# Two reorderings in a hybrid trunk kernel: PSUM copy and decay steps of the CD projections, and the last gated tile of the delta-rule mixer

## The chip, the core and the metric

The kernel runs on one core of a Trainium2 chip. The metric is the device time of one execution in microseconds. The kernel before took 2537.91 us (median of 3 runs, 2536.88 to 2539.83). Engines are named as in the profile: PE multiplies matrices, DVE is the vector engine, ACT the scalar engine, POOL the GpSimd engine, SP issues the DMAs. L840 is line 840 of the kernel.

## What is computed

The reference is a trunk of two residual layers over 1024 tokens of width 1024. Layer 0 mixes with gated delta-rule heads and short gated convolutions (AB), layer 1 with HGRN2 heads and dilated window attention (CD); each layer ends in a SwiGLU block. Two pieces bear on the change. The output of the delta rule is normalised and gated before the output projection, and the gate of HGRN2 is turned into a decay and a key:

```python
o_a = (rms_norm(o_a, norm_g) * silu(z)).reshape(b, t, DN_VW)   # mixer AB
return concatenate([o_a, o_b], axis=-1) @ w_out
f_gate = lb + (1.0 - lb) * sigmoid(hf)                          # mixer CD
log_f = log(f_gate)
k_in = (1.0 - lb) * sigmoid(-hf)
```

With x the projected gate, the kernel uses E = exp(-x), log_f = ln(1 + lb E) - ln(1 + E), and k_in from E and exp(-ln(1 + E)).

## The kernel before

**Arithmetic.** Tokens run along the free axis in two halves of 512. Every large float32 product is made of three matmuls (L135, L136, L137, or L129, L130 and then L132 where the third kind is put last): each operand is split into a high part, a cast on ACT (L102), and the rest, a subtraction on DVE (L103). The third kind reads the low part of the weights, so it is the one that needs the DVE subtraction.

**CD products (`Local.pair`).** The projections of layer 1 are done two output blocks at a time (a "pair" f, 3 to 15) by a seven-product scheme in place of eight. On PE a pair is `p1(f)`, `p2(f)`, `end21(f-1)`, `end12(f-1)`, `p6(f)`, `p5(f)`, `p7(f)`, 12 matmuls each, 84 in all. The order of PE, DVE, ACT, POOL and SP is the order in which the code is written. Each pair needs four weight units: `part_a` for the next pair's p1 and p2 (a11, a12), `part_b` from the weight sums that POOL forms (L335, L336), `part_c` and `part_d` from raw blocks that POOL then combines further (L340, L341). So the DVE split of `part_a(f+1)`, late in pair f, is what the last four matmuls of `p1(f+1)` (L132) wait for.

`copy22(f)` (L878, ACT) copies the PSUM bank x[f], complete when p7(f) ends, into a buffer c; `add22` (L884, DVE) adds another bank to it, and only after the copy may `end21(f)` accumulate on into that bank. The results are then turned by the rotary table: ACT copies the halves crosswise (L859, L860), POOL multiplies (L861), DVE multiplies (L863) and adds (L871). `add11` is L898, `add12` L927, the copies that release the banks are L371 (gt) and L398 (u).

**Decay steps.** For pairs f from 4 to 11 one block of an earlier gate projection goes through `decay(f, 0..7)`: load (SP, L824), clamp (DVE, L829), E = exp(-x) (ACT, L831), two logarithms into c and dy (ACT, L835 and L836, with a load of ACT's function table ahead, attributed to L835), their difference (DVE, L840), exp(-dy) (ACT, L842, again with a table load), a product (DVE, L844), and a running sum (DVE, L847). Steps 0 and 1 are in pair f; before the change steps 2 and 3 are at the end of pair f, step 4 (L840) in pair f+1 behind `part_b`, steps 5 to 7 later in pair f+1. The buffers c come from a pool of two that copy22 and the decay steps share.

**AB, end of the mixer.** `short_conv` projects the convolution branch and calls `tick()` after seven of the eight k-steps of a projection; `tick` counts down and resumes the generator `delta`, which walks through the eight chunks of the delta rule and says with `yield n` how many ticks pass before it is resumed. Its last tiles are `gated(6)` and `gated(7)`: L1851 to L1856 form the scale, L1858 scales the tile (DVE, into dgo), L1861 transposes it on PE in four matmuls, L1865 gates it (DVE), L1866 stores it to DRAM. When short_conv is done, `next(steps)` runs the first 12 matmuls of the output projection of half 0 (k-blocks 4 to 7), then `delta` is run to its end, then the projection goes on. Only PE's order is written out there; a scheduler orders the other engines.

Of the kernel before, what the change touches and what calls it, by code (L numbers as in the profile page):

```python
# [55 lines left out]
def hybrid_trunk_kernel(ctx: ExitStack, tc: tile.TileContext, x_t, w_all, w_down, w_ba, vecs, c_f, c_i, c_rope, out):  # L56
# [33 lines left out]
    def psg():  # L90
        return ps.tile([P, HT], F32, tag="g", name="psg", bufs=2)
# [4 lines left out]
    def psm():  # L96
        return ps.tile([P, HT], F32, tag="m", name="psm", bufs=3)


    def split(hi, lo, src, eng=V):  # L100

        S.copy(hi, src)  # L102
        eng.tensor_tensor(lo, src, hi.bitcast(F32), op=SUB)  # L103

    def unit():

        return ring.tile([P, 2, DM], F32R, tag="w", name="w", bufs=4)
# [180 lines left out]
    class Up:  # L288
# [205 lines left out]
        def pair(self, f, b11, b21, b22, t1, t2, t3, t4):  # L494

            n = f + 1
            self.p1(f, b11)
            self.add22(f - 1)
            an = self.raw("g", n, n % 3 == 1)
            if f == 3:  # L500
                a, b, s = self.w3
                self.sums_late(a, b, s)
                self.combine(0)
                self.part_b(3, s)
                self.combine(1)
            else:
                self.part_d(f, self.a)
                bn = self.raw("u", n, n % 3 == 2)
                self.block_sums()
            self.p2(f, b21, psm())  # L510
            g = self.snap(f)
            if f == 3:
                self.part_c(3, b)
                self.part_d(3, a)
                bn = self.raw("u", n)
            if f > 3:
                self.combine(f - 2)
            self.add11(f, g)
            self.gate11(f)
            if f > 3:  # L520
                self.block_load()
            s = self.sums(an, bn)
            self.end21(f - 1, t4)
            self.part_a(n, an)
            self.sums_late(an, bn, s)
            self.end12(f - 1, b22)
            if f in (5, 7, 9, 11):
                self.block_sums()
            self.late.pop()()
            if f - 1 >= NF // 2:  # L530
                self.ask(f - 1)
            self.p6(f, t2)
            if f in (5, 7, 9, 11):
                self.block_load()
            self.p5(f, t1, psg())
            self.part_b(n, s)
            self.part_c(n, bn)
            self.a = an
            self.p7(f, t3)
# [212 lines left out]
    class Local(Up):  # L752
# [212 lines left out]
        def pair(self, f, last, b11, b21, b22, t1, t2, t3, t4):  # L965

            n = f + 1
            self.p1(f, b11, True)
            self.copy22(f - 1)
            if not last:  # L970
                an = self.raw("g", n, n % 3 == 1)
            else:
                raws = [ring.tile([P, DM], F32, tag="raw", name="raw", bufs=2),
                        self.left.tile([P, DM], F32, tag="spare", name="raw", bufs=1)]
                for raw, j in zip(raws, (8, 9)):
                    dma(raw, w_all[W_AT["cd", j]])
            self.add22(f - 1)
            self.part_b(f, self.s)
            self.sums_late(self.a, self.b, self.s)
            self.decay(f - 1, 4)  # L980
            self.p2(f, b21, psm())
            g = self.snap(f)
            self.rope22(f - 1)
            self.decay(f - 1, 5)
            self.decay(f, 0)
            self.end21(f - 1, t4)
            self.add11(f)
            self.part_c(f, self.b)
            self.rope11(f)
            self.decay(f, 1)  # L990
            self.end12(f - 1, b22)
            self.p6(f, t2)
            self.rope21(f - 1)
            self.part_d(f, self.a)
            self.decay(f - 1, 6)
            if not last:
                bn = self.raw("u", n, n % 3 == 2)
            self.add12(f - 1)
            if not last:
                self.part_a(n, an)  # L1000
            self.decay(f - 1, 7)
            self.store()
            self.p5(f, t1, psg())
            if last:
                self.lead_w = [unit(), unit()]
                for u, raw in zip(self.lead_w, raws):
                    split(u[:, 0, :], u[:, 1, :], raw)
            self.rope12(f - 1)
            if not last:
                self.s = self.sums(an, bn)  # L1010
                self.a, self.b = an, bn
            else:
                self.back = [ring.tile([P, DM], F32, tag="raw", name="raw", bufs=2) for _ in range(2)]
                for i, raw in enumerate(self.back):
                    dma(raw.rearrange("p (k t) -> p k t", k=2), self.b12[:, 2 * i:2 * i + 2, :])
            if f == 3:
                self.bounds()
            self.decay(f, 2)
            self.decay(f, 3)
            self.store()  # L1020
            self.p7(f, t3)

# [295 lines left out]
    def mixer_ab(hn, rb, hp, tr, first, later, second, close, wba, steps):  # L1318
# [102 lines left out]
        with ExitStack() as es:  # L1421
# [291 lines left out]
            def delta(yd, xd, load_al, load_cx):  # L1713
# [132 lines left out]
                def gated(c):  # L1846

                    half, cc = divmod(c, 4)
                    ss = us[c]
                    rq = sca["rq"][:, c, :]  # L1850
                    V.tensor_tensor(ss, ss, rq, op=MULT)  # L1851
                    V.tensor_tensor(ss, ss, rq, op=MULT)
                    V.tensor_scalar(ss, ss, 1.0 / P, EPS, op0=MULT, op1=ADD)
                    rr = bt("rr", [4])
                    G.tensor_tensor(rr, ss, mhalf[:, 0:4], op=ALU.pow)
                    V.tensor_tensor(rr, rr, rq, op=MULT)  # L1856
                    on = bt("dgo", bufs=1)
                    V.tensor_tensor(on, os_all[c], hb(rr), op=MULT)  # L1858
                    o = psm()
                    for h in range(4):  # L1860
                        T.transpose(o[:, h * P:(h + 1) * P], on[:, h, :], ident)  # L1861
                    szc = bt("szc", bufs=1)
                    dma(szc, scr_z[half, :, :, cc * P:(cc + 1) * P])
                    go = bt("dgo", bufs=1)
                    V.scalar_tensor_tensor(go, v4(o), vec[:, R_DNG:R_DNG + 1], szc, op0=MULT, op1=MULT)  # L1865
                    dma(catd[half][0:4, :, cc * P:(cc + 1) * P].rearrange("k p t -> p k t"), go)  # L1866
# [26 lines left out]
                        outputs(c)  # L1893
                    yield 3
                gated(6)
                yield 10
                gated(7)

            def small():


                yield 4
                step(8, 0)
                yield 12
                parts = inverses()
                yield 81
                yield from delta(*parts)
# [15 lines left out]
    def mixer_cd(hn, hp, qkd, wv):  # L1923
# [6 lines left out]
        with ExitStack() as es:  # L1930
# [30 lines left out]
            def hgrn_v(pair, w, tick, tts=range(8)):  # L1961
                def put(tt, o):
                    half, j = divmod(tt, 4)
                    if j == 0:
                        while pair and half and done_c[0] < 3:
                            next(hg_chain)
                        vts[pair, half] = hl("vt", (4, 256), 3)
                    S.copy(vts[pair, half][:, j, :], o)
                v_rows(w, tick, put, tts)
# [711 lines left out]
```

## Time and profile before

| | |
|---|---|
| median of 3 runs | 2537.91 us (2536.88 to 2539.83) |
| the profiled execution | 2542.21 us, span 2540.4 us, clock 0.998 |
| PE busy | 2516.0 us (99%), 13957 matmuls |
| DVE, ACT, POOL busy | 1690.6 (67%), 1081.0 (43%), 649.2 us (26%) |
| DMA moved | 451.48 MB, 178 GB/s on average |

A matmul's busy time in this profile (0.39 us for 512 columns) overlaps its neighbour's. What counts is the distance from one start to the next: 0.227 us where nothing is waited for. A row of the timeline gives start, length, engine, line, operation, output and inputs, and in brackets how long the engine had been idle before and what ended it.

### The profile page before, as it was taken

The numbers are of one execution on the slowest core, as the hardware profiler recorded it, in microseconds if no ns is written. First come the engines' busy times: TensorE is split into PE (matmuls) and PEld (weight loads), VectorE is DVE, ScalarE is ACT, GpSimd is POOL, SyncE is SP. The second block draws the span as 40 slices with busy tenths as digits, with TensorE's granted clock in tenths as the row PEclk, the third lists the DMA queues.
The fourth block names the chain that finished last, engine by engine and source line by source line (L and its number), as shares of the span: only waits on it lengthen the run. The fifth ranks groups of instructions, "written<-read, shape, count | busy, mean of one in ns | idle before, by whom it ended". The sixth has DMA issues, their size and how long they took to land. (4 is left out here: it accounts for less than half of the span.)

```text
span 2540.4 us, 37502 instructions
## 1 busy us (share of the span) xinstructions
PE 2516.0 (99%) x13957; PEld 2083.4 (82%) x13957; DVE 1690.6 (67%) x2858; ACT 1081.0 (43%) x1828; POOL 649.2 (26%) x557
## 2 busy tenths in 40 slices
PE   9999999999999999999999999999999999999998
PEld 7888888888888888888877889888888888888887
DVE  8887786685656565567688666566658565666554
ACT  5422113353333344344676544456645333334442
POOL 0111111343333300033466410000133343330001
PEclk9999999999999999999999999999999999999999
DMA  4435447325556588533344534576742555568753
GB/s 162 155 121 166 131 153 260 113 87 186 183 191 214 202 303 289 187 139 135 126 141 133 187 131 137 152 201 209 234 158 87 177 192 187 203 216 282 278 179 123
DMA packets 281174, 451.48 MB, mean 178 GB/s; under 512 B 49152, under 2 KB 137760, under 8 KB 280736
## 3 DMA queue, kind: packets, MB, share of 16 engines
q1 hardware_dynamic: 280992, 449.10, 53.0%
q8 instruction: 109, 1.79, 0.3%
q14 instruction: 73, 0.60, 0.1%
HBM read 304.74 MB, written 144.26 MB: 177 GB/s over the span
## 5 line engine op out<-in xcount | busy, mean ns | idle before, releaser
L103 DVE TENSOR_TENSOR w<-raw,w 128x1024 fp32r<-128x1024 f32 (+1 forms) x323 | 379.6, 1178 | 129.0 <-ACT w L102 128.5
L102 ACT CAST w<-raw 128x1024 fp32r<-128x1024 f32 (+1 forms) x323 | 306.8, 956 | 268.2 <-PE psu L137 132.9
L135 PE MATMUL psu<-hnh,w 128*128 128x512 f32 x772 | 307.7, 399 | 0.0
L137 PE MATMUL psu<-hnh,w 128*128 128x512 f32 x772 | 301.5, 391 | 0.0
L136 PE MATMUL psu<-hnl,w 128*128 128x512 f32 x772 | 301.1, 390 | 0.0
L196 POOL TENSOR_TENSOR acc<-acc,sq 128x512 f32<-128x512 f32 x52 | 79.4, 1527 | 514.4 <-ACT sq L192 514.3
L335 POOL TENSOR_TENSOR ws<-raw 128x512 f32<-128x512 f32 x54 | 70.6, 1308 | 408.9 <-DMA raw<-in_dram 257.4
L137 PEld LDWEIGHTS psu<-hnh,w 128*128 128x128 f32 x772 | 144.9, 188 | 31.0
L135 PEld LDWEIGHTS psu<-hnh,w 128*128 128x128 f32 x772 | 145.0, 188 | 29.8 <-issue 0.8
L136 PEld LDWEIGHTS psu<-hnl,w 128*128 128x128 f32 x772 | 145.2, 188 | 28.4
L103 DVE TENSOR_TENSOR w<-ws,w 128x1024 fp32r<-128x1024 f32 x51 | 64.7, 1268 | 129.6 <-ACT w L102 129.6
L103 DVE TENSOR_TENSOR hidq<-hr,hidq 128x1024 fp32r<-128x1024 f32 x72 | 82.0, 1141 | 78.7 <-ACT hidq L102 78.6
L102 ACT CAST hidq<-hr 128x1024 fp32r<-128x1024 f32 x72 | 70.3, 980 | 103.1 <-DMA hr<-ts 59.7
L135 PE MATMUL psm<-hidq,w 128*128 128x512 f32 (+1 forms) x275 | 106.1, 386 | 0.0
L136 PE MATMUL psm<-hidq,w 128*128 128x512 f32 (+1 forms) x275 | 105.8, 385 | 0.0
L137 PE MATMUL psm<-hidq,w 128*128 128x512 f32 (+1 forms) x275 | 105.8, 385 | 0.0
L341 POOL TENSOR_TENSOR raw<-raw,ws 128x512 f32<-128x512 f32 x51 | 80.6, 1581 | 60.4 <-DVE w L103 59.2
L135 PE MATMUL psu<-t4h,w 128*128 128x512 f32 x240 | 94.7, 395 | 0.6 <-ACT c L878 0.4
L861 POOL TENSOR_TENSOR sw<-sw,rope 128x512 f32<-128x512 f32 x48 | 72.3, 1506 | 89.5 <-ACT sw L860 68.0
L426 POOL TENSOR_TENSOR hid<-hid,c 128x512 f32<-128x512 f32 x44 | 62.0, 1409 | 125.8 <-ACT hid L425 125.4
L136 PE MATMUL psu<-t4l,w 128*128 128x512 f32 x240 | 93.5, 390 | 0.0
L137 PE MATMUL psu<-t4h,w 128*128 128x512 f32 x240 | 93.5, 389 | 0.0
(548 smaller groups left out, 6787.1 us busy)
## 6 DMA issues: line engine op xcount, KB each, us to landing
raw<-in_dram SPq DMA_DIRECT2D x227, 512.0 KB, 4.3
sd<-in_dram SPq DMA_DIRECT2D x44, 512.0 KB, 4.1
hid<-hid SPq DMA_DIRECT2D x88, 256.0 KB, 3.1
sd<-sd SPq DMA_DIRECT2D x44, 512.0 KB, 3.4
hr<-ts SPq DMA_DIRECT2D x40, 512.0 KB, 4.0
raw<-sd SPq DMA_DIRECT2D x40, 512.0 KB, 4.3
qk<-z SPq DMA_DIRECT2D x52, 256.0 KB, 3.2
hd<-h SPq DMA_DIRECT2D x48, 256.0 KB, 2.8
```

The lines of the kernel that those rows point to most:

```text
L102: S.copy(hi, src)
L103: eng.tensor_tensor(lo, src, hi.bitcast(F32), op=SUB)
L135: T.matmul(o, lh, rh, start=first and i == 0, stop=False, **kw)
L136: T.matmul(o, lh, rl, start=False, stop=False, **kw)
L137: T.matmul(o, ll, rh, start=False, stop=last and i == n - 1, **kw)
L196: (eng or G).tensor_tensor(a, a, q, op=ADD)
L335: G.tensor_tensor(s[:, HT:], b[:, :HT], b[:, HT:], op=ADD)
L341: G.tensor_tensor(a[:, HT:], a[:, HT:], s[:, :HT], op=SUB)
L426: G.tensor_tensor(h, h, self.c22.pop(f), op=MULT)
L861: G.tensor_tensor(sw, sw, self.table[:, 1, t], op=MULT)
```

## The change

In `Local.pair` the decay steps 2 and 3 (exp, table load, two logarithms) leave the end of pair f and come in pair f+1 right behind `copy22(f)`; step 4, the subtraction, moves ahead of the split of `part_b`. In mixer AB, `yield 10` ahead of `gated(7)` becomes `yield 100`: the ticks of short_conv run out first, and the tile comes when `delta` is run to its end.

```diff
@@ Local.pair
             self.p1(f, b11, True)
             self.copy22(f - 1)
+            self.decay(f - 1, 2)
+            self.decay(f - 1, 3)
...
             self.add22(f - 1)
+            self.decay(f - 1, 4)
             self.part_b(f, self.s)
             self.sums_late(self.a, self.b, self.s)
-            self.decay(f - 1, 4)
             self.p2(f, b21, psm())
...
-            self.decay(f, 2)
-            self.decay(f, 3)
             self.store()
             self.p7(f, t3)
@@ mixer_ab, delta
                 gated(6)
-                yield 10
+                yield 100
                 gated(7)
```

**ACT in the CD products.** This is where pair 5 ends and pair 6 begins, before the change; numbers behind names are buffers, and brackets name the engines or queues that an instruction waits for.

```order
L831 ACTIVATE dx_10042<-dx_10042 128x512
L835 ACT_TABLE_LOAD
L835 ACTIVATE c_10140<-dx_10042,lb_9574 128x512 [waits Activation_49]
L836 ACTIVATE dy_10139<-dx_10042 128x512
L878 COPY c_10169<-psu_9996 128x512 [waits DVE_49,PE_49]
L102 CAST w_10175<-ws_10135 128x1024 [waits Pool_49]
```

The same place after the change:

```order
L878 COPY c_10164<-psu_9991 128x512 [waits PE_49]
L831 ACTIVATE dx_10042<-dx_10042 128x512
L835 ACT_TABLE_LOAD [waits DVE_49]
L835 ACTIVATE c_10168<-dx_10042,lb_9574 128x512 [waits Activation_49]
L836 ACTIVATE dy_10167<-dx_10042 128x512
L102 CAST w_10176<-ws_10135 128x1024 [waits Pool_49]
```

The copy went from behind the four decay instructions to ahead of them. The wait for DVE went with the buffer: the copy now gets the buffer c that the last copy used, and the logarithm the one that the last decay used, so the table load ahead of it waits for DVE's running sum (L847) of the decay before.

**DVE in the CD products,** behind add22 of the same pair, as a difference (+ after, - before):

```order
 L863 TENSOR_TENSOR psg<-psg,rope 128x512
 L884 TENSOR_TENSOR psm<-c,psg 128x512
-L103 TENSOR_TENSOR w<-ws,w 128x1024
 L840 TENSOR_TENSOR c<-c,dy 128x512
+L103 TENSOR_TENSOR w<-ws,w 128x1024
 L871 TENSOR_TENSOR z<-psg,sw 128x128x4
 L863 TENSOR_TENSOR psm<-psm,rope 128x512
```

The decay subtraction changed places with the split of part_b. All eight decay pairs change in this way.

**PE at the end of the AB mixer,** before (psu_3863 is short_conv's last projection, psu_3956 the first output projection):

```order
L137 MATMUL psu_3863<-hnh_106,w_2669 128x512
L1861 MATMUL psm_3893<-cf_69,dgo_3891 128x128 [waits DVE_49,PE_49]
L1861 MATMUL psm_3893<-cf_69,dgo_3891 128x128 x3
L135 MATMUL psu_3863<-hnh_106,w_2669 128x512
L136 MATMUL psu_3863<-hnl_107,w_2669 128x512
L137 MATMUL psu_3863<-hnh_106,w_2669 128x512
L135 MATMUL psu_3956<-hnh_3910,w_3946 128x512
```

After (psu_3938 is the first output projection):

```order
L135 MATMUL psu_3938<-hnh_3892,w_3928 128x512
L136 MATMUL psu_3938<-hnl_3893,w_3928 128x512
L137 MATMUL psu_3938<-hnh_3892,w_3928 128x512
L1861 MATMUL psm_3959<-cf_69,dgo_3957 128x128 [waits DVE_49,PE_49]
L1861 MATMUL psm_3959<-cf_69,dgo_3957 128x128 x3
L135 MATMUL psu_3938<-hnh_3910,w_3928 128x512
```

The four transposes of gated(7) come 15 matmuls later: behind the last three of short_conv and the 12 of the output projection's first part. On DVE the gating of the tile (L1865) falls behind the convolution's output (L1537), one weight split and two operand splits; on SP its store (L1866) falls behind the convolution's store and a weight load, directly ahead of the eight loads of the residual (L176), and of the operand loads of half 1 (L1288) the third comes behind a store of the residual (L252) that it was ahead of.

## The prediction

> **What bounds the kernel now.** I read the page first, for the engine that has no room:
>
> ```profile
> PE 2516.0 (99%) x13957; PEld 2083.4 (82%) x13957; DVE 1690.6 (67%) x2858; ACT 1081.0 (43%) x1828; POOL 649.2 (26%) x557
> ```
>
> PE is busy 99% of the span and the change neither adds nor removes an instruction on any engine, so it can win only where PE stands still. The view of PE's waits has two rows at the changed places:
>
> ```profile
> PE psm L1861 <- DVE dgo L1858: 0.7, 1, 0.7
> PE psu L132 <- DVE w L103: 1.1, 4, 0.4
> ```
>
> The first is gated(7), the second the low-weight matmuls of p1 in the CD pairs. A wait row only counts what is idle beyond a matmul's modelled end, so it understates; the distance of starts tells more. The timeline of PE gives the first matmul of p1 of pairs 5, 6, 14 and 15:
>
> ```profile
> 1221.47 0.39 PE L129 MATMUL psu<-hnh,w 128*128 128x512 f32 x1
> 1240.51 0.39 PE L129 MATMUL psu<-hnh,w 128*128 128x512 f32 x1
> 1398.17 0.39 PE L129 MATMUL psu<-hnh,w 128*128 128x512 f32 x1
> 1417.21 0.39 PE L129 MATMUL psu<-hnh,w 128*128 128x512 f32 x1
> ```
>
> Pair 14 has no decay and takes 1417.21 - 1398.17 = 19.04 us, 0.2267 for each of its 84 matmuls. Pair 5 takes 19.04 too, with decay steps beside it, so these don't slow the matmuls as such. The eight pairs 6 to 13 take 157.66 us, and 8 x 19.04 = 152.32: **5.34 us are lost there**, 0.67 a pair. This is the most that the CD part can give.
>
> What sets those pairs is a round of the other engines. ACT in pair 8 (p1 begins at 1280.30):
>
> ```profile
> 1281.87 0.58 ACT L860 COPY sw<-psg 64x512 f32<-64x512 f32 x1
> 1282.48 0.63 ACT L831 ACTIVATE dx<-dx 128x512 f32<-128x512 f32 x1
> 1285.05 0.61 ACT L836 ACTIVATE dy<-dx 128x512 f32<-128x512 f32 x1
> 1285.57 0.57 ACT L878 COPY c<-psu 128x512 f32<-128x512 f32 x1
> 1287.20 1.05 ACT L102 CAST w<-ws 128x1024 fp32r<-128x1024 f32 x1 [1.06 <-POOL ws L336]
> 1289.35 0.58 ACT L860 COPY sw<-psm 64x512 f32<-64x512 f32 x1
> 1291.29 1.28 ACT L842 ACT_TABLE_LOAD   x1 [1.35 <-DVE c L840]
> 1293.12 1.03 ACT L102 CAST w<-raw 128x1024 fp32r<-128x1024 f32 x1
> ```
>
> DVE and POOL in the same pair:
>
> ```profile
> 1282.24 1.21 DVE L847 TENSOR_TENSOR_SCAN dy<-rmask,c 128x512 f32<-128x512 f32 x1
> 1284.28 0.75 DVE L863 TENSOR_TENSOR psg<-psg,rope 128x512 f32<-128x512 f32 x1
> 1286.17 0.70 DVE L884 TENSOR_TENSOR psm<-c,psg 128x512 f32<-128x512 f32 x1 [1.14 <-ACT c L878]
> 1288.29 1.23 DVE L103 TENSOR_TENSOR w<-ws,w 128x1024 fp32r<-128x1024 f32 x1 [1.42 <-ACT w L102]
> 1289.43 1.78 DVE L840 TENSOR_TENSOR c<-c,dy 128x512 f32<-128x512 f32 x1
> 1292.72 0.68 DVE L898 TENSOR_TENSOR psm<-psm,gt 128x512 f32<-128x512 f32 x1
> 1294.18 1.23 DVE L103 TENSOR_TENSOR w<-raw,w 128x1024 fp32r<-128x1024 f32 x1 [0.79 <-ACT w L102]
> 1298.90 0.69 DVE L103 TENSOR_TENSOR w<-raw,w 128x512 fp32r<-128x512 f32 x1
> 1300.76 1.23 DVE L103 TENSOR_TENSOR w<-raw,w 128x1024 fp32r<-128x1024 f32 x1
> ...
> 1285.87 1.30 POOL L336 TENSOR_TENSOR ws<-ws,raw 128x512 f32<-128x512 f32 x1
> 1287.12 1.31 POOL L340 TENSOR_TENSOR raw<-raw 128x512 f32<-128x512 f32 x1
> 1288.38 2.29 POOL L341 TENSOR_TENSOR raw<-raw,ws 128x512 f32<-128x512 f32 x1
> ```
>
> Followed forward: part_b's cast (1287.20) waits for POOL's sums; DVE splits it, then runs L840 until 1291.21; only then may ACT load the table for L842, after an idle 1.35 us; then comes part_c's cast, whose split (1294.18) DVE has waited 0.79 us for. From there DVE runs without a break to part_a's split, which ends at 1301.99. PE wants it eight matmuls after p1 began at 1299.95, at 1301.76, and got it later:
>
> ```profile
> 1301.53 0.39 PE L130 MATMUL psu<-hnl,w 128*128 128x512 f32 x1
> 1302.04 1.20 PE L132 MATMUL psu<-hnh,w 128*128 128x512 f32 x4
> ```
>
> The start is 0.28 us late; restarting and the other late spot (end21 behind the copy L878, done at 1286.14) make up the rest of the 0.67.
>
> **CD, step by step.** *Copy ahead of the decay steps.* After L860 (1282.45) the copy comes first, to 1283.02; everything in front of the second logarithm moves 0.57 later, and that ends at 1286.2 instead of 1285.66. Behind it stands part_b's cast, which waits for POOL until 1287.20 anyway: its idle 1.06 us pays for the 0.57, at no cost. L884 then runs when DVE is through with L863 (1285.03), 1.14 earlier, and end21 no longer waits for the copy.
>
> *L840 ahead of part_b's split.* It may start at 1286.25, in time in which DVE idles now. It needs 0.6 to 1.8 us: 0.69 is what a split of the same size with both inputs in SBUF takes while POOL is idle (1298.90), 1.78 what L840 takes behind POOL's L341, which itself takes 2.29 against 1.31 for L340. In either case it ends before 1288.1, ahead of the cast's end at 1288.25. L842's table load then follows L860 at 1289.94 instead of 1291.29: **1.35 us off the round.** Part_c's cast ends 1292.8 instead of 1294.15.
>
> *What is late next.* Part_b's split may be held behind L340, which L840 has pushed back: between 0 and the 1.30 us of one such POOL operation; I take 0.6, so that it ends at 1290.1. Two operations on, L898 ends 2.2 us later (as now from L840's end at 1291.21 to 1293.40), at 1292.3, still ahead of part_c's cast. At the other end, 1.30, it would be 1293.0, and 1.15 of the 1.35 would be left. So the 1.35 arrive at part_a's split. The round took 19.7 us a pair and can then do 18.3; PE needs 19.04 and becomes the bound. In pair 14 the same last stretch, fed by PE's own p6, ends this much ahead of need:
>
> ```profile
> 1416.21 1.21 DVE L103 TENSOR_TENSOR w<-raw,w 128x1024 fp32r<-128x1024 f32 x1
> 1419.03 1.07 PE L132 MATMUL psu<-hnh,w 128*128 128x512 f32 x4
> ```
>
> 1419.03 - 1417.42 = 1.6 us; a decay pair has the product L844 and the clamp L829 in that stretch as well, about 0.8 together by the split's 0.69 as the nearest size, which leaves 0.8. I expect no stall at L132, and book 5.0 of the 5.34 us, leaving 0.3 for single late starts that the pattern doesn't show. Bounds: 5.34 if nothing stays; 0 if another link of the round is as long as the one cut; below nothing only by the new wait under the rivals.
>
> A rule of the Trainium skill speaks against this place: "SBUF — State Buffer", section "Who interferes with whom", says that a DVE instruction with two SBUF inputs and a GpSimd instruction that reads SBUF exclude each other for a whole instruction. The trace agrees, with L840 at 1.78 us where 0.69 would do. By the rule the harm depends on who comes first: an L840 that gets in ahead of L336 holds the sums, and part_b's cast, by 0.69. That leaves 0.66 of the 1.35, about what PE loses per pair; it is the rival "half" below.
>
> **AB.** PE and DVE at gated(7):
>
> ```profile
> 405.84 0.74 DVE L1530 SCALAR_TENSOR_TENSOR sca<-cs,vec,sca 128x512 f32<-128x512 f32 x1
> 406.50 0.68 DVE L1858 TENSOR_TENSOR dgo<-os,rr 128x512 f32<-128x512 f32 x1
> ...
> 406.26 0.39 PE L137 MATMUL psu<-hnh,w 128*128 128x512 f32 x1
> 407.33 0.63 PE L1861 MATMUL psm<-cf,dgo 128*128 128x128 f32 x4 [0.68 <-DVE dgo L1858]
> ```
>
> The transposes start 1.07 us after the matmul ahead of them, 0.84 more than 0.227. Fifteen matmuls later PE reaches them at 406.49 + 15 x 0.227 = 409.9, and L1858, whose place on DVE is the same, ended at 407.18: **0.84 us** go. The cost of the transposes themselves stays.
>
> What moves with them is on DVE and SP. L1865 goes from 408.97 to about 412.1 behind its new neighbours, its store to 412.8, and the residual loads queued behind that store on SP move from 412.50 to about 413.2:
>
> ```profile
> 412.50 4.07 SPq L176 DMA_DIRECT2D h<-in_dram  x8
> 416.64 0.69 DVE L1312 TENSOR_TENSOR h<-h,psu 128x512 f32<-128x512 f32 x1 [0.20 <-DMA h<-in_dram]
> 431.82 1.23 DVE L103 TENSOR_TENSOR w<-raw,w 128x1024 fp32r<-128x1024 f32 x1
> 435.69 0.39 PE L135 MATMUL psg<-hnh,w 128*128 128x512 f32 x1
> ```
>
> The first addition (L1312) then starts near 417.3, in time in which DVE would wait for the next product. The operand load of half 1 that falls behind a residual store (L1288) comes perhaps 2 us later and holds DVE in order; the next weight split (431.82, ending at 433.05) serves the matmuls of 435.69, which come 0.84 earlier: 1.8 us of room. Cover lost there would cost PE the difference, at most some 0.5 us. I take 0.8 for AB, between 0.3 and 0.84.
>
> **Sum.** 5.0 + 0.8 = 5.8 us. The profiled execution took 2542.21 us, 1.81 of it outside the span of 2540.4, and becomes 2536.4. It stands 4.30 above the median of the runs; taking the same off 2537.91 gives **2532.1 us**. Whoever adds the two upper bounds gets 6.18 and 2531.7.
>
> **Rivals.**
> *Half (0.17).* DVE and POOL take back what the order gives: L840 gets in ahead of L336, part_b's cast slips by 0.69, and stalls of some 0.3 us a pair remain. For it speaks that L840's new time, 1286.25, is close to L336's start; against it that L336 starts first, at 1285.87. 5.34 / 2 + 0.8 = 3.5: 2534.4.
> *CD does nothing (0.12).* Another link, such as the raw block that feeds the sums, is equally long; then the table load waits elsewhere and L132 as before. Pair 14, whose PE loses nothing with the same loads, speaks against it. Only AB's 0.8 remain: 2537.1.
> *Slower (0.05).* The logarithm's table load now waits for DVE's running sum L847, which ends at 1283.45, and that load is due at 1283.67: 0.2 us of room. ACT works in order, so a late L847 holds part_b's cast and all behind it. Room of 1.0 ahead of the cast and the 1.35 gained have to be used up first; from an L847 that ends 2.4 us later on, each further 0.5 costs eight times 0.5: 2541. Since L847 stands right behind part_a's split, which comes earlier, not later, I give it little.
> *The forecast (0.66).* Between 2531.0 and 2533.5, with the scatter of a median of few runs of about 1 us.
>
> A measurement of this kernel can tell about 0.2% from no change, 5.1 us: the line lies at 2532.8, 0.7 above my forecast. Of the 0.66 some 0.49 falls below it, and nearly nothing of the rest: faster 0.50; same 0.46; slower 0.04. Range 2530.7 to 2535.8: it takes in the forecast's spread and the half case, and leaves out the last two.
>
> **What would show it.** Right: in pairs 6 to 13 p1 begins every 19.04 us; L842's table load follows L860 with no idle time for L840; L884 starts straight behind L863; the transposes of gated(7) start 0.23 us after the matmul ahead of them. Wrong: pairs stay above 19.3; an idle time ahead of L835's table load (by L847) or a longer one ahead of part_b's cast; L840 or part_b's split near 2.5 us; a new gap of PE between 408 and 445.

## The result, and the profile after the change

The changed kernel takes 2533.66 us (median of 18 runs, 2532.65 to 2536.38), the kernel before 2539.09 (18 runs, 2536.32 to 2544.23). The ratio is 0.998, with a 95% interval of 0.9972 to 0.9987: **5.1 us faster, between 3.3 and 7.1**.

The page of the changed kernel has the same number of instructions on PE, which is again busy for 99% of a span that is now 2531.5 us:

```profile
PE 2510.7 (99%) x13957; PEld 2083.7 (82%) x13957; DVE 1699.0 (67%) x2858; ACT 1082.0 (43%) x1828; POOL 648.4 (26%) x557
```

The timeline of PE shows the first matmul of p1 in pairs 6 and 14:

```profile
1240.29 0.39 PE L129 MATMUL psu<-hnh,w 128*128 128x512 f32 x1
1392.61 0.39 PE L129 MATMUL psu<-hnh,w 128*128 128x512 f32 x1
```

The eight decay pairs take 152.32 us, which is 8 x 19.04 to the hundredth. All of the 5.34 us are gone. This is how ACT now goes through pair 8 (p1 begins at 1278.37):

```profile
1279.68 0.59 ACT L878 COPY c<-psu 128x512 f32<-128x512 f32 x1
1280.16 0.63 ACT L831 ACTIVATE dx<-dx 128x512 f32<-128x512 f32 x1
1280.81 1.28 ACT L835 ACT_TABLE_LOAD   x1
...
1284.29 1.06 ACT L102 CAST w<-ws 128x1024 fp32r<-128x1024 f32 x1 [0.94 <-POOL ws L336]
1286.45 0.58 ACT L860 COPY sw<-psm 64x512 f32<-64x512 f32 x1
1287.05 1.28 ACT L842 ACT_TABLE_LOAD   x1
...
1292.17 0.59 ACT L398 COPY u<-psu 128x512 f32<-128x512 f32 x1 [1.05 <-PE psu L137]
```

Four things are to be seen. The copy L878 stands first, and the cast of part_b still waits 0.94 us for POOL: the copy has only used up idle time. The table load of L842 starts 0.02 us after L860 ends, with no bracket behind it: the wait of 1.35 us for L840 is gone. The table load of L835, which now waits for the running sum L847, follows L831 without a gap: the new wait costs nothing. And L398 waits 1.05 us for PE, where in the kernel before it had no wait in this pair: now PE sets the pace of the helpers. DVE and POOL in the same pair:

```profile
1279.16 1.21 DVE L847 TENSOR_TENSOR_SCAN dy<-rmask,c 128x512 f32<-128x512 f32 x1
...
1281.87 0.69 DVE L884 TENSOR_TENSOR psm<-c,psg 128x512 f32<-128x512 f32 x1
1283.39 1.42 DVE L840 TENSOR_TENSOR c<-c,dy 128x512 f32<-128x512 f32 x1 [0.82 <-ACT dy L836]
1285.38 1.66 DVE L103 TENSOR_TENSOR w<-ws,w 128x1024 fp32r<-128x1024 f32 x1 [0.57 <-ACT w L102]
...
1289.95 1.23 DVE L103 TENSOR_TENSOR w<-raw,w 128x1024 fp32r<-128x1024 f32 x1 [0.71 <-ACT w L102]
1297.07 1.21 DVE L103 TENSOR_TENSOR w<-raw,w 128x1024 fp32r<-128x1024 f32 x1
...
1282.96 1.30 POOL L336 TENSOR_TENSOR ws<-ws,raw 128x512 f32<-128x512 f32 x1
1284.21 1.74 POOL L340 TENSOR_TENSOR raw<-raw 128x512 f32<-128x512 f32 x1
```

L840 runs in the 2.8 us between L884 and part_b's split, in which DVE has nothing else. The last row of DVE, part_a's split, ends at 1298.28. PE uses it here, in the timeline of PE:

```profile
1299.00 0.39 PE L130 MATMUL psu<-hnl,w 128*128 128x512 f32 x1
1299.22 1.07 PE L132 MATMUL psu<-hnh,w 128*128 128x512 f32 x4
```

The split is ready 0.94 us early, and L132 starts 0.22 us after the matmul ahead of it, where it took 0.51 before.

At the end of the AB mixer PE goes through the moved transposes without a stop, and the residual's first addition on DVE comes later than before:

```profile
410.25 0.39 PE L137 MATMUL psu<-hnh,w 128*128 128x512 f32 x1
410.48 0.60 PE L1861 MATMUL psm<-cf,dgo 128*128 128x128 f32 x4
435.44 0.39 PE L135 MATMUL psg<-hnh,w 128*128 128x512 f32 x1
...
418.31 0.69 DVE L1312 TENSOR_TENSOR h<-h,psu 128x512 f32<-128x512 f32 x1 [2.12 <-DMA h<-in_dram]
432.79 1.22 DVE L103 TENSOR_TENSOR w<-raw,w 128x1024 fp32r<-128x1024 f32 x1
```

The two profiled spans differ by 2540.4 - 2531.5 = 8.9 us, more than the change. Of these, 5.34 are the pairs and 0.84 gated(7). The rest is a stall that neither edit touches. PE waits at the same place in both kernels, some 320 us behind the last decay pair, for a cause that the profile calls "issue". In the timeline of PE of the kernel before:

```profile
1720.25 0.40 PE L136 MATMUL psu<-t1l,w 128*128 128x512 f32 x1
1722.88 0.80 PE L137 MATMUL psu<-t1h,w 128*128 128x512 f32 x1 [2.23 <-issue]
```

In that of the changed kernel the same matmul waits 0.16 us:

```profile
1715.15 0.50 PE L137 MATMUL psu<-t1h,w 128*128 128x512 f32 x1 [0.16 <-issue]
```

This is worth about 2.1 us. For the next 3.2 us the matmuls before came 0.43 us apart instead of 0.227, about 1.4 us more. The starting phase of the changed kernel, in turn, was 0.6 us slower. Together, 5.34 + 0.84 + 2.1 + 1.4 - 0.6 = 9.1. Whoever subtracts spans credits the change with accidents; the medians of eighteen runs do so far less.

### The profile page after: what moved, and what is told of

It reads as the page before. It is cut to its first block, busy times and chain, and to the rows that moved or that the text cites. A ratio compares the mean times of both kernels' runs of the same rounds, so it can differ in the third digit from the quotient of the medians.

```text
span 2531.5 us, 37501 instructions
## 1 busy us (share of the span) xinstructions
PE 2510.7 (99%) x13957; PEld 2083.7 (82%) x13957; DVE 1699.0 (67%) x2858; ACT 1082.0 (43%) x1828; POOL 648.4 (26%) x557
## 4 chain that ended last, share of the span: by engine, by line
PE 83%; DVE 7%; ACT 2%; issue 1%; DMA 1%; POOL 1%; SPq 0%; POOLq 0%; DVEq 0%; ACTq 0%
PE psu L135 15%; PE psu L137 15%; PE psu L136 15%; PE psg L135 6%; PE psg L137 6%; PE psg L136 6%; PE psm L135 5%; PE psm L136 5%; PE psm L137 5%; PE psm L2286 1%; DVE h L258 1%; DVE h L625 1%; DVE w L103 1%; PE psu L129 1%; DVE w L322 1%
## 5 line engine op out<-in xcount | busy, mean ns | idle before, releaser
L103 DVE TENSOR_TENSOR w<-raw,w 128x1024 fp32r<-128x1024 f32 (+1 forms) x323 | 386.2, 1198 | 128.3 <-ACT w L102 127.1
L335 POOL TENSOR_TENSOR ws<-raw 128x512 f32<-128x512 f32 x54 | 70.1, 1299 | 406.9 <-DMA raw<-in_dram 269.6
L135 PE MATMUL psu<-t3h,w 128*128 128x512 f32 x240 | 93.4, 389 | 0.0
```

Of the source, the lines that this page charges most:

```text
L135: T.matmul(o, lh, rh, start=first and i == 0, stop=False, **kw)
L335: G.tensor_tensor(s[:, HT:], b[:, :HT], b[:, HT:], op=ADD)
```

## The experiments

The theory at stake is the prediction's: **the round**. The chain from part_b's cast over L840, the table load of L842 and part_c's cast to part_a's split took longer than PE's 19.04 us; L840's new place shortens it, the copy's costs nothing, and PE is the bound. It is a round because its end feeds its start: L927, on DVE directly ahead of part_a's split, lets ACT copy the halves crosswise (L859, L860), for which POOL's product L861 waits, and behind that POOL forms the sums (L335 at 1284.50, then L336) for part_b's cast. In pair 8 of the kernel before:

```profile
1281.28 0.58 ACT L859 COPY sw<-psg 64x512 f32<-64x512 f32 x1 [1.69 <-DVE psg L927]
...
1282.53 2.01 POOL L861 TENSOR_TENSOR sw<-sw,rope 128x512 f32<-128x512 f32 x1 [3.16 <-ACT sw L860]
```

The rival is **the copy**: the late copy L878 holds L884 and end21, so the gain comes from its move. A third question is whether 19.04 is a limit of PE with slack behind it or only another link of a chain.

**The two parts apart.** *cd_only* has the CD products of the changed kernel and the AB mixer of before:

```
                 gated(6)
-                yield 100
+                yield 10
                 gated(7)
```

> The CD edits alone. Both theories of the CD part (round: ACT waited 1.35 us for L840 in each pair; copy: end21 and add22 waited for a late copy) expect pairs 6 to 13 at 19.04 us each, 152.3 us in all instead of 157.7, and the 0.84 us stall of PE at gated(7) back. Time: 5.3 us below before, 0.2%. If a large part of the 5.4 us between the medians came from AB, this run stays within 3 us of before. The start-up of PE and the 2.2 us stall of PE named issue near 1720 us, followed by 3.2 us at a granted clock of 0.50, that before's profile has and after's has not: if it belongs to one execution and not to the change, it may stand here or not.

*ab_only* has the AB mixer of the changed kernel and the CD products of before:

```
                 gated(6)
-                yield 10
+                yield 100
                 gated(7)
```

> The AB edit alone. Prediction: 0.84 us go at gated(7), whose transposes start 0.23 us after the matmul ahead of them; nothing else moves, pairs 6 to 13 still take 157.7 us. Time: 0.8 us below before, less than can be told from no change. Rival: the later residual loads and the changed order of DMAs cost PE a stall between 408 and 460 us that takes the 0.84 back.

Against 2539.18 us before (33 runs), cd_only took 2534.48 us, ratio 0.998 (0.9971 to 0.9989), and ab_only 2538.11 us, ratio 0.9997 (0.9988 to 1.0006; 11 runs each). Nearly all of the gain is CD's, whose eight pairs take 152.32 us in cd_only; AB alone can't be told from no change. The two together (0.998 x 0.9997 = 0.9977) give what the whole change gives, within these intervals, so nothing shows that the parts work on each other. The timeline of PE shows what the AB edit does all the same. First gated(7) in cd_only, with the old AB order:

```profile
406.45 0.39 PE L137 MATMUL psu<-hnh,w 128*128 128x512 f32 x1
406.84 0.63 PE L1861 MATMUL psm<-cf,dgo 128*128 128x128 f32 x4
```

Then in ab_only, with the new one:

```profile
410.62 0.39 PE L137 MATMUL psu<-hnh,w 128*128 128x512 f32 x1
410.85 0.60 PE L1861 MATMUL psm<-cf,dgo 128*128 128x128 f32 x4
```

The stall is 0.16 us in the first and nothing in the second. In five executions with the old order it was 0.16, 0.26, 0.53, 0.84 and 1.01, 0.56 on average; the 0.84 of the prediction was one draw. The rival of ab_only, a new gap of PE between 408 and 460 us, is not there: over the same 260 matmuls up to L208 near 463 us PE takes 59.44 us in the kernel before and 58.61 in ab_only and in the changed kernel, 0.83 less.

ab_only also showed that the pairs had been mis-sized. Its first matmuls of p1 in pairs 6 and 14, CD being as before:

```profile
1240.64 0.39 PE L129 MATMUL psu<-hnh,w 128*128 128x512 f32 x1
1396.55 0.39 PE L129 MATMUL psu<-hnh,w 128*128 128x512 f32 x1
```

These are 155.91 us: 3.59 lost and not 5.34, since the pairs start to stall only from pair 8 on.

**The two moves of CD apart.** *sub_only* is the kernel before with L840 alone moved:

```
             self.add22(f - 1)
+            self.decay(f - 1, 4)
             self.part_b(f, self.s)
             self.sums_late(self.a, self.b, self.s)
-            self.decay(f - 1, 4)
```

> Only the subtraction L840 moved ahead of part_b's split; exp and logarithms stay at the end of pair f, ahead of the copy. Round theory: ACT no longer idles 1.35 us ahead of L842, PE's wait at L132 goes, pairs 6 to 13 take 19.04 to 19.2 us (152.3 to 153.6 in all); what may remain is end21 behind the late copy, 0.1 to 0.15 a pair. Copy theory: pairs stay at 19.6 to 19.7. Time: 4 to 5.3 us below before by the first, 0 to 0.5 by the second.

*copy_only* is the kernel before with the copy alone moved ahead of the logarithms:

```
             self.copy22(f - 1)
+            self.decay(f - 1, 2)
+            self.decay(f - 1, 3)
...
-            self.decay(f, 2)
-            self.decay(f, 3)
             self.store()
```

> Only the copy moved ahead of exp and logarithms; the subtraction L840 stays behind part_b's split. Round theory: ACT still idles about 1.35 us ahead of L842, PE still waits at L132, pairs 6 to 13 take 19.5 to 19.7 us (156.5 to 157.7 in all); the start of end21 behind the copy is the only thing won, at most 1.1 us in all. Copy theory: pairs at 19.04. Time: 0 to 1.1 us below before by the first, 5.3 by the second.

sub_only took 2535.3 us, ratio 0.9984 (0.9975 to 0.9993), copy_only 2539.93 us, ratio 1.0001 (0.9993 to 1.001). The timeline of PE in sub_only, first p1 matmuls of pairs 6 and 14, and ACT's table load:

```profile
1243.84 0.39 PE L129 MATMUL psu<-hnh,w 128*128 128x512 f32 x1
1396.16 0.39 PE L129 MATMUL psu<-hnh,w 128*128 128x512 f32 x1
...
1309.45 1.28 ACT L842 ACT_TABLE_LOAD   x1
```

152.32 us again, nothing lost, and no wait at the table load; even the small rest at end21 that I had expected is not there. In copy_only the waits of ACT still have the old row, with 1.35 us for each of the eight pairs, and PE loses 3.69 us:

```profile
  DVE c L840: 10.8, 8
```

**The copy theory falls.** Moving L840 alone takes away the whole loss of the pairs; moving the copy brings no gain that these runs can see. It does take away a stop of PE, and that is instructive. In pair 10 of the kernel before, PE's starts are 0.53 us apart ahead of the first L132 and 0.27 and 0.34 at the start of end21, instead of 0.227. In copy_only the stop at end21 is gone, and the one at L132 has grown to 0.73: the pair takes 19.69 us, where it took 19.67. As long as the round sets the time, a stop that is removed from PE comes back at the next wait.

**The size of the loss before.** *before_again* is the kernel before, unchanged, for another profile.

> The kernel before once more, for the scatter of single executions. If the size of a spot is the program's, it is as in the first profile: 5.34 us lost in pairs 6 to 13, 0.84 at gated(7), 2.2 at the stall named issue near 1720 us. If it is the execution's, pairs lose between 3.6 and 5.3, gated(7) between 0.2 and 1.0 and the issue stall between 0.2 and 2.8, as the four part runs have them with the same code at these spots.

It took 2537.95 us, and its pairs lost 3.65 us, with stalls at L132 only from pair 8 on. What the first profile had beyond that begins with one load. The view of POOL in the kernel before, and of its issue on SP:

```profile
1218.57 0.33 SPq L308 DMA_DIRECT2D raw<-in_dram  x1
...
1225.34 1.29 POOL L335 TENSOR_TENSOR ws<-raw 128x512 f32<-128x512 f32 x1 [13.60 <-DMA raw<-in_dram]
```

The same sum in before_again:

```profile
1219.04 0.33 SPq L308 DMA_DIRECT2D raw<-in_dram  x1
...
1223.40 1.29 POOL L335 TENSOR_TENSOR ws<-raw 128x512 f32<-128x512 f32 x1 [11.52 <-DMA raw<-in_dram]
```

The block was issued at 1218.57 and used 6.8 us later; in before_again it was issued at 1219.04 and used 4.4 us later. Such a late block delays the round from the start. A round that is longer than PE's pair never makes the delay good, and PE loses 0.84 us and 0.87 in pairs 6 and 7 already, which cost at most 0.05 each in the other three executions with L840 in its old place. In sub_only the same block was as late, issued at 1221.90 and used at 1228.67, 6.8 us later, and no pair lost anything: the shorter round makes the delay good. That the late load alone makes the 1.7 us between 5.34 and 3.65 was not tried by a run of its own.

**How much room the round has.** In *spin1*, *spin2* and *spin3* the changed kernel copies `dy` once, twice or three times onto itself ahead of L842, inside the round. The diff of spin2:

```
                 elif step == 5:
+                    for _ in range(2):
+                        S.copy(y, y)
                     S.activation(y, y, AF.Exp, scale=-1.0)
```

> The changed kernel with one more ACT copy (dy onto itself, about 0.6 us) ahead of exp(-dy) in each decay pair: a known length put into the round at the place where L840's wait stood. Round theory: the round takes 18.3 us by the prediction, 18.9 with the copy, still under PE's 19.04: pairs 6 to 13 stay at 19.04, 152.3 in all. If the round is only just covered, each pair loses up to 0.6, 157 in all.

> The same with two copies, 1.2 us, nearly what the wait for L840 was. Round theory: 18.3 + 1.2 = 19.5, so the stall at L132 is back with about 0.4 us in each pair once the slack is used up, 153 to 156 in all. If the round has nothing to do with it, PE stays at 152.3.

> The same with three copies, 1.8 us. Round theory: 18.3 + 1.8 = 20.1, about 1 us lost in each pair once the slack is used up, 157 to 161 in all: each further copy costs its own length. If the round has nothing to do with it, PE stays at 152.3.

They took 2533.79, 2538.66 and 2545.32 us, one execution each, beside 2538.08 for the kernel before. The p1 matmuls of pairs 6 and 14 in spin1:

```profile
1239.75 0.39 PE L129 MATMUL psu<-hnh,w 128*128 128x512 f32 x1
1392.07 0.39 PE L129 MATMUL psu<-hnh,w 128*128 128x512 f32 x1
```

In spin2, those of pairs 6, 10, 13 and 14, with the two copies that ACT makes in a pair (named L843 in this file):

```profile
1240.37 0.39 PE L129 MATMUL psu<-hnh,w 128*128 128x512 f32 x1
1317.52 0.39 PE L129 MATMUL psu<-hnh,w 128*128 128x512 f32 x1
1376.49 0.39 PE L129 MATMUL psu<-hnh,w 128*128 128x512 f32 x1
1396.19 0.39 PE L129 MATMUL psu<-hnh,w 128*128 128x512 f32 x1
...
1327.38 1.28 ACT L843 COPY dy<-dy 128x512 f32<-128x512 f32 x2
```

In spin3, the same four, and the row of L132, which is back among the waits of PE:

```profile
1240.57 0.39 PE L129 MATMUL psu<-hnh,w 128*128 128x512 f32 x1
1319.80 0.50 PE L129 MATMUL psu<-hnh,w 128*128 128x512 f32 x1
1380.69 0.50 PE L129 MATMUL psu<-hnh,w 128*128 128x512 f32 x1
1400.77 0.39 PE L129 MATMUL psu<-hnh,w 128*128 128x512 f32 x1
...
PE psu L132 <- DVE w L103: 3.8, 7, 0.6
```

The eight pairs take 152.32, 155.82 and 160.20 us. The first copy is free. From pair 10 to pair 13, where the delay has built up, a pair takes (1376.49 - 1317.52) / 3 = 19.66 us with two copies and (1380.69 - 1319.80) / 3 = 20.30 with three: 0.64 for the copy, its own duration. This is the signature of a round that is the bound. Counted back by the same 0.64 for each copy, 19.66 - 1.28 = **18.38 us is the round of the changed kernel**, and with one copy it is 19.02, just under PE's 19.04. Both are estimates, since PE hides a round that is shorter than its own pair; that the first copy is free agrees with them. This answers the third question: 19.04 is PE's own limit, and the round has about 0.66 us of room below it. Two copies, 1.28 us, put back about what the old place of L840 cost (1.35), and PE loses 3.50 us, much as in the kernel before.

## Why the prediction was right

**Where PE lost time.** Right in place, too large in size: 5.34 us was what one profiled execution lost, and three others with L840 in its old place (before_again, ab_only, copy_only) lost 3.59 to 3.69. The size was read off an execution that stood 4.30 us above its median, and 1.69 of these (5.34 - 3.65, against before_again, which stood at the median) were the pairs' own surplus; the sum took the 4.30 off the result and left the surplus in the gain.

**Copy ahead of the decay steps, at no cost.** Right: in copy_only it costs nothing and in sub_only its absence costs nothing. That it also frees L884 and end21 is true and unneeded, as the round, once short enough, leaves them time.

**L840 into DVE's idle time.** Right: it ends at 1284.81, before the cast (1285.35), and L842's table load waits no longer. This was the step that carried the gain, and sub_only shows it alone. L840's duration, forecast between 0.6 and 1.8, has its row in the view by lines of the changed kernel (shortest, median and longest, in ns):

```profile
L840 DVE TENSOR_TENSOR c<-c,dy x8: 1050/1511/1522, 1225.2 to 1359.3; 128x512 f32<-128x512 f32 x8
```

The same view of the kernel before:

```profile
L840 DVE TENSOR_TENSOR c<-c,dy x8: 1771/1780/1783, 1230.3 to 1368.2; 128x512 f32<-128x512 f32 x8
```

**Part_b's split held behind POOL.** Right in kind: 1.66 us instead of 1.23, so it was held 0.43 where I took 0.6, while L340 went from 1.31 to 1.74. In all eight pairs L840 started behind L336 and not ahead of it, so the sums were not held, and the rival "half" did not come. Its length went with what was left of L336: 1.51 us where it started 0.32 behind L336 (1302.16 and 1301.84), 1.05 where it started 0.80 behind (1225.16 and 1224.36). The section "Who interferes with whom" of the Trainium skill's "SBUF — State Buffer", which the prediction weighed, fits these rows. The same hold came at a place that the prediction does not list: the small split that took 0.69 us at 1298.90 now starts 0.60 behind POOL's L861 (1294.64 and 1294.04) and takes 1.25. The prediction calls POOL idle at 1298.90; L861 still ran for the first 0.12 us there. No run took POOL's work away, so this step is read from the rows and not tested.

**The round and what bounds next.** Right: 18.38 us by the spins for the forecast 18.3; slack at L132 0.94 us for the forecast 0.8; pairs at exactly 19.04. Of the two operations that the forecast took off pair 14's 1.6 us, only L844 (0.66 from its start to the next) lies in the stretch that PE feeds; L829 stands ahead of it. And the 0.94 is not the room of the round: in spin1, whose round is 0.64 longer, the split is ready just as early (it ends at 1297.73, L132 starts at 1298.68). It measures the last stretch alone, which starts from PE's p6; the room of the round is the 0.66 us that the spins give.

**AB.** The transposes follow after 0.23 us as forecast. They came at 410.48 instead of 409.9, as the starting phase of this execution was 0.6 us slower. The first addition came at 418.31, 1 us later than forecast, and the weight split behind it (ending at 434.01) still had 1.4 us of room to the matmul at 435.44. There is no new gap of PE there, as the 260 matmuls above show. The term was booked at 0.8, between 0.3 and 0.84; five executions put it between 0.16 and 1.01, at 0.56.

**The sum.** I booked 5.8 us. With the sizes seen over several executions it is 3.65 + 0.56 = 4.2; the runs say 5.1, between 3.3 and 7.1, which holds both, and cannot say which is nearer. So that the time came out this close to the sum is in part luck. One reason for more than 4.2 is visible: an execution with the old order can lose 5.34, and its 18 runs spread over 7.9 us, those of the changed kernel over 3.7. The 2532.1 us stands 1.6 below the measured median; of that, 1.2 is that the kernel before itself came out at 2539.09 and not at 2537.91.

**The rivals.** The measured 2533.66 lies inside the range, but 0.16 above the window 2531.0 to 2533.5 that was given 0.66, and nearer to the 2534.4 of "half" than to the forecast's 2532.1. The time alone does not decide for the mechanism; the traces do. "CD does nothing" and "half" are excluded by the 152.32 us, "slower" by the table load of L835, which has no idle time ahead of it: in pair 8 L847 ended at 1280.37, 0.4 us before L831 did.

## What to carry to other kernels

When a saturated engine waits a few tenths of a microsecond for a helper, follow the helpers' round and not the wait: here PE waited for a split on DVE, that was late by a table load on ACT, and this waited for a subtraction that DVE did one place too late. Put the operation that another engine waits for ahead of one that nobody waits for yet, and check with deliberate delays, one at a time, how much room the round has gained. A stall that recurs by a chain with no slack depends on when the chain is first delayed, so size it from several executions, and compare profiles stage by stage, since their spans differ by stalls that have nothing to do with the change.

## What the runs showed of the hardware that I had not expected

The "issue" stall near 1720 us stands at the same matmul, at the step from t1's low to its high part, in every profile taken, and lasts between 0.2 and 2.8 us: 2.2 in the kernel before, 0.2 in the changed one, 1.7 in cd_only, 0.4 in ab_only, 0.9 in sub_only, 2.8 in copy_only, 0.5 to 0.6 in the other four. With the whole gain at some 5 us, it alone can blur a comparison of two profiles. In the kernel before, the view by stretches has the clock that the throttle granted behind it (columns: stretch, length, busy time and count of PE, PEld, DVE, ACT and POOL, granted clock, DMA share, GB/s):

```profile
1718.00:1722.80 4.80, 2.65 (x134) 1.81 (x133) 3.48 (x11) 1.75 (x6) 0.00 (x0) 0.98 0.92 277
1722.80:1726.00 3.20, 3.12 (x7) 2.51 (x8) 2.67 (x10) 1.20 (x2) 0.00 (x0) 0.50 0.37 126
```

The DMA share is 0.92 around the stall, and the granted clock falls to 0.50 for 3.2 us after it. The clock did not fall after the 2.8 us of copy_only or the 1.7 us of cd_only, so the length of the stall alone does not decide it. What causes the stall, the busy transfers or something else, was not tested and stays open.
